# Gate pass of a hybrid decoder trunk: the skip's factor on GpSimd, and weight splits one half step later

## The chip, the cores and the metric

The kernel runs on one core of a Trainium2 chip. The metric is the device time of one execution in microseconds (us). A core has TensorE (PE, with its weight loads as PEld), VectorE (DVE), ScalarE (ACT), GpSimd (POOL) and SyncE (SP). Each runs its own list of instructions in a fixed order, and semaphores make one engine wait for another. In this kernel SP and ACT issue the DMAs.

## The reference

One layer on x of 4096 x 1024 float32. After an RMSNorm, one projection gives five streams; two head groups use them, and a second projection joins them.

```python
u = rmsnorm(x, norm_w)
pool_x, pool_z, m_x, m_z, m_o = split(u @ w_in)            # 1024 columns each
y_pool = pool_mixer(pool_x) * silu(pool_z)
xc = silu(causal_conv(m_x));  h = mlstm_chunkwise(...)     # 4 heads of 256
h  = sigmoid(m_o) * h
hn = (h - mean(h)) * rsqrt(var(h) + EPS) * mh_norm_w       # per head
y_mlstm = (hn + m_skip * xc) * silu(m_z)
out = rmsnorm(x + concat(y_pool, y_mlstm) @ w_out)
```

The edit touches `m_skip * xc` and the preparation of the weights of the large products.

## The kernel before

The kernel has three stages: the pooling group (to about 755 us), the mLSTM (to about 1727 us), and a function `drive` that runs four *block-product passes*. The passes are, in order, `p_out1` (the pooling half of the output projection, to 2062 us), `p_o` (the *gate pass*, m_o, to about 2464 us), `p_z` (m_z, to about 2768 us) and `p_out2` (the mLSTM half of the output projection). Each pass is a product by Strassen's scheme with NP = 7 block products. It goes over NR = 4 rows r of 1024 positions; in each r over the seven products i, and in each product over two *half steps* kh. One half step is 24 matmuls, three for each product of a float32 pair, because every operand is split into a rounded high part and the rest: `split` casts on ScalarE (L104) and subtracts on VectorE (L105). A pass has 56 half steps.

In a half step `drive` issues the load of a later left operand (sr, L212, on ACT's queue), splits the one loaded before (L104, L105), emits the 24 matmuls (L111 to L113), lets each item finish with the product's result, and runs what has been deferred. `defer(fn, n)` puts `fn` on a list, and `run_deferred` counts it down once in each half step and runs it when n reaches zero. `load` allocates a weight's slot, issues the DMA of its sums (L161; a raw block is loaded by L154 before) and defers its split by one half step. This happens for the weights missing in the first r of the first pass, and in the last r of each pass for the next pass's seven.

In the gate pass, Head items make h for 128 positions and 512 channels: the gate's Tanh on ACT (L1067), times h (L1069, DVE), statistics (L1076, L1077, DVE), then for two items together rs = var + 4 EPS (L1082, DVE), its power -1/2 (L1083, POOL), nb = -mean x rs (L1085, DVE), and the normalisation h x rs + nb in place (L1090, ACT, four per pair). When a quarter of r is done, `heads_ready` gives four pairs of functions, one for each block of 128 channels. `fetch` loads xc into a tile of the ring xu (L1107, SP) and defers its multiplication by the channel's skip (L1108); `finish`, later, transposes the normalised h on PE (L1115) and adds the two on DVE (L1117: transposed x mh_norm_w + skip part). The result is stored by L184. Besides, `right_sums` makes sums of the next pass's weights: four loads (L132, SP), four additions on POOL (L138, L140, L143, L145), in r = 0 to 2 of the gate pass.

The program's order on each engine is not written by hand: a scheduler places the instructions on each engine by its own estimate, so the order after an edit is read from the built program. Within an engine's list nothing overtakes.

Of the kernel before, what the change touches and what calls it, by code (L numbers as in the profile page):

```python
# [11 lines left out]
AF = mybir.ActivationFunctionType  # L12
ALU = mybir.AluOpType
# [41 lines left out]
def tile_hybrid(  # L55
# [16 lines left out]
    nc = tc.nc  # L72
# [17 lines left out]
    msk = col[:, 56:64]  # L90
# [12 lines left out]
    def split(raw, hi, lo, eng=None):  # L103
        nc.scalar.copy(out=hi, in_=raw)  # L104
        (eng or nc.vector).tensor_tensor(out=lo, in0=raw, in1=hi.bitcast(F32), op=ALU.subtract)  # L105

    def mm3(ps, pairs, start=True, stop=True, skip=False):

        n = len(pairs)
        for k, (a, b) in enumerate(pairs):  # L110
            nc.tensor.matmul(ps, lhsT=a[0], rhs=b[0], start=start and k == 0, stop=False, skip_group_check=skip)  # L111
            nc.tensor.matmul(ps, lhsT=a[0], rhs=b[1], start=False, stop=False, skip_group_check=skip)  # L112
            nc.tensor.matmul(ps, lhsT=a[1], rhs=b[0], start=False, stop=stop and k == n - 1, skip_group_check=skip)  # L113
# [56 lines left out]
    def defer(fn, n=1):  # L170
        deferred.append([n, fn])

    def run_deferred():
        due = []
        for d in deferred:
            d[0] -= 1
            if d[0] <= 0:
                due.append(d)
        for d in due:
            deferred.remove(d)  # L180
            d[1]()

    def store(dst, t):
        defer(lambda: nc.sync.dma_start(out=dst, in_=t))  # L184
# [15 lines left out]
    def drive(passes, ring, slot_pool, tile, psp, background, first):  # L200


        steps = [(n, r, i, kh) for n in range(len(passes)) for r in range(NR) for i in range(NP) for kh in range(2)]
        got = {}

        def issue(t):
            if t >= len(steps):
                return
            n, r, i, kh = steps[t]
            hi = ring.tile([P, 2, T], F32R, name="sr")  # L210
            lo = ring.tile([P, 2, T], F32R, name="sr")
            nc.scalar.dma_start(out=lo.bitcast(F32), in_=passes[n].left[r][i][:, 2 * kh:2 * kh + 2, :])  # L212
            got[t] = hi, lo

        def make(t):
            if len(first) <= t < len(steps):
                hi, lo = got[t]
                split(lo.bitcast(F32), hi, lo)

        def load(p, i):  # L220
            def splits(todo):
                for f in todo:
                    f()

            todo = p.load(i, *slot_pool(i))
            defer(lambda: splits(todo))


        later, fetched = [], []
        banks = {}  # L230

        def prefetch():
            while later and len(fetched) < 4:
                get, use = later.pop(0)
                get()
                fetched.append(use)

        for t, pairs in enumerate(first):
            got[t] = tuple([pair[v] for pair in pairs] for v in range(2))
        assert len(first) == AHEAD - 1  # L240
        for t, (n, r, i, kh) in enumerate(steps):
            p = passes[n]
            issue(t + AHEAD - 1)
            if n + r == 0:
                miss = [v for v in range(NP) if v not in p.slots]
                if miss:
                    p.fetch(miss[0], tile)
                    load(p, miss[0])
            make(t + AHEAD - 2)
            s = got.pop(t)  # L250
            w = p.slots[i]
            if kh == 0 and i in (0, 1, 4):
                for q in range(4):
                    banks["abc"[(0, 1, 4).index(i)], q] = psp.tile([P, T], F32, name="ps")
            chain = "abab" "cbc"[i]
            if t % 14 == 0:
                for it in p.items:
                    it.begin(r)
            for q in range(4):
                ps = banks[chain, q]  # L260
                pairs = []
                for k in range(2):
                    kk = 2 * kh + k
                    sk = tuple(z[k] if isinstance(z, list) else z[:, k] for z in s)
                    if p.by_row:
                        pairs.append((tuple(z[:, q * P:(q + 1) * P] for z in sk), tuple(z[:, kk, :] for z in w)))
                    else:
                        pairs.append((tuple(z[:, kk, q * P:(q + 1) * P] for z in w), sk))
                mm3(ps, pairs, start=kh == 0 and i in (0, 1, 4), stop=kh == 1, skip=True)
                if kh == 1:  # L270
                    p.items[q].after(r, i, ps)
            if kh == 1:
                later.extend(p.ready(r, i) or ())
            run_deferred()
            if r + 1 == NR and n + 1 < len(passes):
                if kh == 0 and i:
                    load(passes[n + 1], i - 1)
                if kh == 1 and i < NP - 1 or (kh, i) == (0, NP - 1):
                    passes[n + 1].fetch(i, tile)
                if kh == 1 and i == NP - 1:  # L280
                    load(passes[n + 1], i)
            m = t % 14
            if m in FREE_BANKS:
                for _ in range(FREE_BANKS[m]):
                    if fetched:
                        fetched.pop(0)()
            prefetch()
            background(n, r, m)
        while later or fetched:
            prefetch()  # L290
            run_deferred()
            fetched.pop(0)()
        while deferred:
            run_deferred()
# [85 lines left out]
    with tc.tile_pool(name="a_st", bufs=4) as stp, \  # L380
# [147 lines left out]
        for b in range(NB):  # L528
# [6 lines left out]
            for j in range(NJ):  # L535
# [22 lines left out]
                if b == 0:  # L558
# [4 lines left out]
                                               op0=ALU.mult, op1=ALU.subtract)  # L563
# [22 lines left out]
    with tc.tile_pool(name="b_mx", bufs=NJ) as mxp, \  # L586
# [7 lines left out]
        def x_tile(dt=F32):  # L594
            return xu.tile([P, T], dt, name="xu")
# [404 lines left out]
    with tc.tile_pool(name="c_ring", bufs=8) as ring, \  # L1000
# [8 lines left out]
        class Sum(Item):  # L1009
# [5 lines left out]
            def get(self, r, rh, ch):  # L1015
                t = self.tile()
                nc.sync.dma_start(out=t, in_=self.src[rows_of(r, rh, self.q), ch * T:(ch + 1) * T])
                return t
# [74 lines left out]
        def heads_ready(r, i):  # L1093

            if i not in (2, 4, 5, 6):
                return
            rh, ch = {2: (0, 0), 4: (1, 1), 5: (1, 0), 6: (0, 1)}[i]
            name = {2: "c11", 4: "u3", 5: "s1", 6: "u2"}[i]
            hn = [getattr(it, name) for it in p_o.items]

            def turned(jj):
                j = 4 * ch + jj
                got = []

                def fetch():
                    sk = x_tile()
                    nc.sync.dma_start(out=sk, in_=xc_d[2 * r + rh][j])  # L1107
                    defer(lambda: nc.scalar.activation(out=sk, in_=sk, func=AF.Copy, scale=msk[:, j:j + 1]))  # L1108
                    got.append(sk)

                def finish():
                    sk, = got
                    tp = psp.tile([P, T], F32, name="ps")
                    for q in range(NCH):
                        nc.tensor.transpose(out=tp[:, q * P:(q + 1) * P], in_=hn[q][:, jj * P:(jj + 1) * P],  # L1115
                                            identity=ident)
                    nc.vector.scalar_tensor_tensor(out=sk, in0=tp, scalar=mhw[:, j:j + 1], in1=sk,  # L1117
                                                   op0=ALU.mult, op1=ALU.add)
                    store(hs_d[2 * r + rh][j], sk)

                return fetch, finish

            return [turned(jj) for jj in range(4)]
# [79 lines left out]
        def slot_pool(i):  # L1203
            return (w1p, "w1") if i < 4 else (w2p, "w2")
# [34 lines left out]
        def background(n, r, m):  # L1239
            if (n, r) == (0, 1) and m in (1, 3, 5, 7, 9, 11) or (n, r) == (0, 2) and m in (1, 3):  # L1240
                next(more)
            if n < 3 and m in (((2, 5, 8, 11), (), (6, 9, 11, 13), ()) if n == 0 else
                               ((1, 4, 7, 10), (1, 4), (1, 4), ()))[r]:
                next(weights[n])
            if (n, r, m) == (3, 0, 2):
                for h in range(2):
                    fw.append(x_tile())
                    nc.sync.dma_start(out=fw[h], in_=final_w[:, h * T:(h + 1) * T].partition_broadcast(P))
# [57 lines left out]
```

## Time and profile before

| what | value |
|---|---|
| median of 3 runs | 3108.35 us (3103.76 to 3109.62) |
| the profiled execution | 3106.23 us |
| its span | 3104.5 us |
| granted TensorE clock, mean | 0.972 |
| busy: PE, DVE, ACT, POOL | 2903.6, 2116.8, 1352.9, 883.5 us |
| TensorE's busy time, 1727.7 to 2062 (`p_out1`) | 309.08 of 334.30 us |
| 2062 to 2446 (gate pass) | 349.93 of 384 us |
| 2446 to 2768 (`p_z` and the gate pass's end) | 313.17 of 322 us |
| 2768 to 3093 (`p_out2`) | 310.26 of 325 us |

A row of the timeline gives the start, the duration, the engine and line, output <- input, how many instructions are joined in it, and in brackets how long the engine was idle before and what released it. A row of the waits gives the engine and what it wanted, what it waited for, and the total, the number and the longest of the waits. The sum of the profiled execution's idle and busy time is its span; the remaining 1.7 us lie around it.

### The profile page before, as it was taken

The numbers are of one execution on the slowest core, as the hardware profiler recorded it, in microseconds if no ns is written. First come the engines' busy times: TensorE is split into PE (matmuls) and PEld (weight loads), VectorE is DVE, ScalarE is ACT, GpSimd is POOL, SyncE is SP. The second block draws the span as 40 slices with busy tenths as digits, with TensorE's granted clock in tenths as the row PEclk, the third lists the DMA queues.
The fourth block names the chain that finished last, engine by engine and source line by source line (L and its number), as shares of the span: only waits on it lengthen the run. The fifth ranks groups of instructions, "written<-read, shape, count | busy, mean of one in ns | idle before, by whom it ended". The sixth has DMA issues, their size and how long they took to land. (4 is left out here: it accounts for less than half of the span.)

```text
span 3104.5 us, 45002 instructions
## 1 busy us (share of the span) xinstructions
PE 2903.6 (94%) x15912; PEld 2520.3 (81%) x15912; DVE 2116.8 (68%) x4172; ACT 1352.9 (44%) x2658; POOL 883.5 (28%) x924
## 2 busy tenths in 40 slices
PE   7999999998899999999998898998999999989998
PEld 6888888887889989989997676886777778867887
DVE  6555555554688888888889644567667766676666
ACT  4222122221676676767767311245556633343332
POOL 1122333333244454444443231002011133220000
PEclk9999999998999999999999999999999999999999
DMA  6344455546221121111212788676677888886664
GB/s 214 113 158 157 160 186 187 186 149 199 82 67 50 49 69 49 61 57 48 66 59 92 250 281 288 218 256 218 228 238 247 268 270 279 277 285 207 202 210 169
DMA packets 258002, 531.59 MB, mean 171 GB/s; under 512 B 28528, under 2 KB 72048, under 8 KB 257776
## 3 DMA queue, kind: packets, MB, share of 16 engines
q1 hardware_dynamic: 225952, 412.84, 38.4%
q10 hardware_dynamic: 31824, 115.88, 12.2%
q8 instruction: 125, 2.05, 0.3%
q14 instruction: 101, 0.83, 0.1%
HBM read 331.49 MB, written 197.13 MB: 170 GB/s over the span
## 5 line engine op out<-in xcount | busy, mean ns | idle before, releaser
L111 PE MATMUL ps<-w,sr 128*128 128x512 f32 x1320 | 523.5, 397 | 27.0 <-ACT sr L104 18.5
L113 PE MATMUL ps<-w,sr 128*128 128x512 f32 x1320 | 520.4, 395 | 18.5 <-DVE sr L105 18.5
L112 PE MATMUL ps<-w,sr 128*128 128x512 f32 x1320 | 521.1, 395 | 0.0
L105 DVE TENSOR_TENSOR sr<-sr 128x1024 fp32r<-128x1024 f32 x221 | 284.9, 1292 | 302.2 <-ACT sr L104 301.5
L104 ACT CAST sr<-sr 128x1024 fp32r<-128x1024 f32 x221 | 231.2, 1047 | 535.0 <-PE ps L112 255.3
L111 PE MATMUL acc<-u,w 128*128 128x512 f32 x1024 | 399.3, 390 | 1.6 <-ACT u L104 1.6
L112 PE MATMUL acc<-u,w 128*128 128x512 f32 x1024 | 399.3, 390 | 0.0
L113 PE MATMUL acc<-u,w 128*128 128x512 f32 x1024 | 399.2, 390 | 0.0
L111 PEld LDWEIGHTS ps<-w,sr 128*128 128x128 f32 x1320 | 252.3, 191 | 82.2 <-ACT sr L104 22.3
L113 PEld LDWEIGHTS ps<-w,sr 128*128 128x128 f32 x1320 | 251.3, 190 | 74.5 <-DVE sr L105 22.2
L111 PE MATMUL acc<-xu,w 128*128 128x256 f32 x992 | 296.4, 299 | 0.0
L112 PEld LDWEIGHTS ps<-w,sr 128*128 128x128 f32 x1320 | 251.7, 191 | 52.4 <-issue 0.5
L113 PE MATMUL acc<-xu,w 128*128 128x256 f32 x992 | 283.3, 286 | 0.0
L112 PE MATMUL acc<-xu,w 128*128 128x256 f32 x992 | 283.3, 286 | 0.0
L666 POOL TENSOR_TENSOR cs<-c,cs 128x516 fp32r<-128x516 f32 x124 | 179.8, 1450 | 240.0 <-ACT cs L665 214.4
L678 DVE SCALAR_TENSOR_TENSOR xc<-mx,col,xc 128x256 f32<-128x256 f32 x384 | 226.2, 642 | 15.2 <-ACT xc L760 11.5
L111 PEld LDWEIGHTS acc<-u,w 128*128 128x128 f32 x1024 | 192.3, 188 | 42.3 <-ACT u L104 2.4
L113 PEld LDWEIGHTS acc<-u,w 128*128 128x128 f32 x1024 | 192.4, 188 | 40.1
L112 PEld LDWEIGHTS acc<-u,w 128*128 128x128 f32 x1024 | 192.4, 188 | 40.0
L111 PEld LDWEIGHTS acc<-xu,w 128*128 128x128 f32 x992 | 192.7, 194 | 1.2
L112 PEld LDWEIGHTS acc<-xu,w 128*128 128x128 f32 x992 | 192.8, 194 | 0.0
L113 PEld LDWEIGHTS acc<-xu,w 128*128 128x128 f32 x992 | 192.2, 194 | 0.1
(230 smaller groups left out, 5927.9 us busy)
## 6 DMA issues: line engine op xcount, KB each, us to landing
sr<-us_d ACTq DMA_DIRECT2D x112, 512.0 KB, 5.1
us_d<-st SPq DMA_DIRECT2D x64, 512.0 KB, 2.7
sr<-ym_d ACTq DMA_DIRECT2D x56, 512.0 KB, 4.3
sr<-yp_d ACTq DMA_DIRECT2D x53, 512.0 KB, 5.6
st<-in_x_t_dram SPq DMA_DIRECT2D x32, 512.0 KB, 6.0
yp_d<-sg SPq DMA_DIRECT2D x64, 256.0 KB, 2.9
st<-us_d SPq DMA_DIRECT2D x32, 512.0 KB, 5.9
xu<-us_d SPq DMA_DIRECT2D x64, 256.0 KB, 3.6
```

Source lines behind the costliest of these rows:

```text
L104: nc.scalar.copy(out=hi, in_=raw)
L105: (eng or nc.vector).tensor_tensor(out=lo, in0=raw, in1=hi.bitcast(F32), op=ALU.subtract)
L111: nc.tensor.matmul(ps, lhsT=a[0], rhs=b[0], start=start and k == 0, stop=False, skip_group_check=skip)
L112: nc.tensor.matmul(ps, lhsT=a[0], rhs=b[1], start=False, stop=False, skip_group_check=skip)
L113: nc.tensor.matmul(ps, lhsT=a[1], rhs=b[0], start=False, stop=stop and k == n - 1, skip_group_check=skip)
L666: nc.gpsimd.tensor_tensor(out=t[:, 1], in0=cst[h], in1=t[:, 0].bitcast(F32), op=ALU.subtract)
L678: nc.vector.scalar_tensor_tensor(out=a[:, t], in0=m[:, t, i:i + TB], scalar=conv_w[:, jj * 4 + i:jj * 4 + i + 1], in1=a[:, t], op0=ALU.mul ...
```

## The change

The skip's multiplication L1108 (64 instructions in the gate pass) goes from ScalarE to GpSimd, and the deferred split of a weight runs two half steps after its load is issued instead of one. Nothing else is edited. Lines after the skip's grow by one (L1117 is L1118 in the changed kernel).

```diff
             todo = p.load(i, *slot_pool(i))
-            defer(lambda: splits(todo))
+            defer(lambda: splits(todo), 2)
...
                     nc.sync.dma_start(out=sk, in_=xc_d[2 * r + rh][j])
-                    defer(lambda: nc.scalar.activation(out=sk, in_=sk, func=AF.Copy, scale=msk[:, j:j + 1]))
+                    defer(lambda: nc.gpsimd.tensor_scalar(out=sk, in0=sk, scalar1=msk[:, j:j + 1], scalar2=None,
+                                                          op0=ALU.mult))
                     got.append(sk)
```

On GpSimd, in r = 1 of the gate pass (xu is the tile of skip x xc, rs the variance whose power is taken; + stands in the changed kernel alone, the other rows in both):

```order
 L1083 TENSOR_TENSOR rs_22523<-rs_22523,nhalf_70 128x4
+L1108 TENSOR_SCALAR xu_22714<-xu_22714,col_68 128x512
+L1108 TENSOR_SCALAR xu_22716<-xu_22716,col_68 128x512
 L1083 TENSOR_TENSOR rs_22611<-rs_22611,nhalf_70 128x4
+L1108 TENSOR_SCALAR xu_22718<-xu_22718,col_68 128x512
+L1108 TENSOR_SCALAR xu_22720<-xu_22720,col_68 128x512
 L1083 TENSOR_TENSOR rs_22652<-rs_22652,nhalf_70 128x4
+L1108 TENSOR_SCALAR xu_22828<-xu_22828,col_68 128x512
+L1108 TENSOR_SCALAR xu_22830<-xu_22830,col_68 128x512
+L1108 TENSOR_SCALAR xu_22832<-xu_22832,col_68 128x512
+L1108 TENSOR_SCALAR xu_22879<-xu_22879,col_68 128x512
 L1083 TENSOR_TENSOR rs_22756<-rs_22756,nhalf_70 128x4
```

Between two powers there now stand two or four skip factors, and r = 0 and r = 2 have the same rows with other numbers.

On ScalarE at the same place, before:

```order
L1090 ACTIVATE ch_22038<-ch_22038,nb_22614,rs_22611 128x256 x2
L1090 ACTIVATE ch_22046<-ch_22046,nb_22614,rs_22611 128x256 x2
L1067 ACTIVATE ch_22062<-ch_22062 128x512
L104 CAST sr_22661<-sr_22662 128x1024
L1108 ACTIVATE xu_22714<-xu_22714,col_68 128x512
L1108 ACTIVATE xu_22716<-xu_22716,col_68 128x512
L1108 ACTIVATE xu_22718<-xu_22718,col_68 128x512
L212 DMA sr_22835<-us_d2_74 128x1024
L1108 ACTIVATE xu_22720<-xu_22720,col_68 128x512
L1067 ACTIVATE ch_22148<-ch_22148 128x512
L1090 ACTIVATE ch_22054<-ch_22054,nb_22655,rs_22652 128x256 x2
L1090 ACTIVATE ch_22062<-ch_22062,nb_22655,rs_22652 128x256 x2
```

and on ScalarE there after the change:

```order
L1067 ACTIVATE ch_22062<-ch_22062 128x512
L1090 ACTIVATE ch_22038<-ch_22038,nb_22614,rs_22611 128x256 x2
L1090 ACTIVATE ch_22046<-ch_22046,nb_22614,rs_22611 128x256 x2
L104 CAST sr_22661<-sr_22662 128x1024
L212 DMA sr_22835<-us_d2_74 128x1024
L1090 ACTIVATE ch_22054<-ch_22054,nb_22655,rs_22652 128x256 x2
L1090 ACTIVATE ch_22062<-ch_22062,nb_22655,rs_22652 128x256 x2
```

The four skip factors are gone from between the two normalisations, and a Tanh stands ahead of the first.

On VectorE between the two nb of this group, before (the L1117 are the sums behind earlier transposes, sr a left operand's split):

```order
L1085 SCALAR_TENSOR_TENSOR nb_22614<-mv_22590,rs_22611 128x4
L1076 BN_STATS stats_22631<-ch_22054 128x6
L1077 BN_AGGR mv_22590<-stats_22631 128x2
L105 TENSOR_TENSOR sr_22574<-sr_22574,sr_22573 128x1024
L1077 BN_AGGR mv_22590<-stats_22631 128x2
L1117 SCALAR_TENSOR_TENSOR xu_22532<-ps_22690,col_68,xu_22532 128x512
L1117 SCALAR_TENSOR_TENSOR xu_22534<-ps_22696,col_68,xu_22534 128x512
L1069 SCALAR_TENSOR_TENSOR ch_22062<-ch_22062,xu_22513 128x512
```

and on VectorE after:

```order
L1085 SCALAR_TENSOR_TENSOR nb_22614<-mv_22590,rs_22611 128x4
L1077 BN_AGGR mv_22590<-stats_22631 128x2 x2
L105 TENSOR_TENSOR sr_22574<-sr_22574,sr_22573 128x1024
L1069 SCALAR_TENSOR_TENSOR ch_22062<-ch_22062,xu_22513 128x512
L1118 SCALAR_TENSOR_TENSOR xu_22532<-ps_22690,col_68,xu_22532 128x512
```

L1069 now stands ahead of both sums; nb stays ahead of the subtraction of sr and of L1069. Further down, the subtraction of the next sr (sr_22662) went from ahead of the second power's L1082 to behind the second nb.

On VectorE at the start of the first pass (w_ is a weight, L1026 adds a product to rows of x):

```order
+L105 TENSOR_TENSOR sr<-sr 128x1024
+L1026 TENSOR_TENSOR ch<-ps,ch 128x512 x12
 L105 TENSOR_TENSOR w_18892<-w_18892,w_18891 128x1024 x2
 L105 TENSOR_TENSOR sr<-sr 128x1024
-L1026 TENSOR_TENSOR ch<-ps,ch 128x512 x12
-L105 TENSOR_TENSOR w_18955<-w_18955,w_18954 128x1024
-L105 TENSOR_TENSOR sr<-sr 128x1024
-L105 TENSOR_TENSOR w_18955<-w_18955,w_18954 128x1024
-L105 TENSOR_TENSOR sr<-sr 128x1024
```

The twelve L1026 now come ahead of the two halves of a weight, where before the next weight's halves stood behind them with a left operand's split between.

## The prediction

> **What bounds the kernel now.** I read the page's head first, then the stretches of the block-product passes, then the waits of the gate pass and the timeline where TensorE stops in it.
>
> ```profile
> PE 2903.6 (94%) x15912; PEld 2520.3 (81%) x15912; DVE 2116.8 (68%) x4172; ACT 1352.9 (44%) x2658; POOL 883.5 (28%) x924
> ```
>
> TensorE is busy 94% of the span, so no edit here can win more than TensorE's idle time, and none can cost more than it makes TensorE wait. The gate pass runs from about 2062 to 2464 us; the windows below are two stretches of it, each about as long as one r (us, PE busy, PEld, DVE, ACT, POOL, granted clock, DMA share, GB/s).
>
> ```profile
> 2160.00:2255.00 95.00, 86.77 (x400) 71.98 (x399) 64.09 (x138) 49.70 (x81) 14.43 (x12) 0.96 0.69 227
> 2255.00:2352.00 97.00, 86.57 (x397) 71.70 (x396) 64.93 (x148) 51.58 (x83) 14.07 (x12) 0.95 0.71 232
> ```
>
> 8 to 10 us of each are TensorE's idle time; ScalarE is half idle, GpSimd nearly empty. No engine's load sets the time here; the order of dependent steps does. The waits between 2062 and 2446 us (total, times, longest) and the skip factor's own groups say which:
>
> ```profile
> POOL rs L1083 <- DVE rs L1082: 165.2, 16, 32.8
> ACT ch L1090 <- DVE nb L1085: 57.6, 23, 7.2
> DVE nb L1085 <- POOL rs L1083: 35.4, 30, 6.1
> PE ps L1115 <- ACT ch L1090: 27.1, 14, 5.6
> L1108 ACT ACTIVATE xu<-xu,col x64: 706/718/741, 2035.4 to 2465.3; 128x512 f32<-128x512 f32 x64
>   DMA xu<-xc_d: 40.2, 15
> DMA to landing us min/median/max: 2.6/4.8/7.7
> ```
>
> TensorE's stops are nearly all transposes (L1115) waiting for the normalisation (L1090): 27.1 us. That hangs on nb (L1085), which hangs on the power on GpSimd (L1083). The last three lines are the skip factor: 64 x 0.718 = 46 us of ScalarE, and 40.2 us in which ScalarE stood before it because its input, loaded by L1107, takes 4.8 us to land.
>
> **Moving the skip factor.** ScalarE loses 46 us of work and 40.2 us of waiting. GpSimd gets both, and GpSimd is where the power stands. So the order on GpSimd decides, not its load. It has two skip factors ahead of rs_22611 and two ahead of rs_22652, where before the powers followed each other directly. The r = 1 group before, ScalarE, then GpSimd, SyncE, VectorE and TensorE:
>
> ```profile
> 2244.66 1.95 ACT L1108 ACTIVATE xu<-xu,col 128x512 f32<-128x512 f32 x3
> 2249.86 0.72 ACT L1108 ACTIVATE xu<-xu,col 128x512 f32<-128x512 f32 x1 [3.25 <-DMA xu<-xc_d]
> 2251.00 2.06 ACT L1090 ACTIVATE ch<-ch,nb,rs 128x256 f32<-128x256 f32 x4
> ...
> 2239.98 1.01 POOL L1083 TENSOR_TENSOR rs<-rs,nhalf 128x4 f32<-128x4 f32 x1 [7.35 <-DVE rs L1082]
> 2248.18 1.01 POOL L1083 TENSOR_TENSOR rs<-rs,nhalf 128x4 f32<-128x4 f32 x1 [7.19 <-DVE rs L1082]
> 2266.07 1.26 POOL L145 TENSOR_TENSOR xu<-xu 128x512 f32<-128x512 f32 x1
> ...
> 2236.39 3.03 SPq L1107 DMA_DIRECT2D xu<-xc_d  x3
> 2244.72 0.32 SPq L1107 DMA_DIRECT2D xu<-xc_d  x1
> ...
> 2241.02 0.16 DVE L1085 SCALAR_TENSOR_TENSOR nb<-mv,rs 128x4 f32<-128x4 f32 x1 [0.88 <-POOL rs L1083]
> 2242.72 1.38 DVE L1117 SCALAR_TENSOR_TENSOR xu<-ps,col,xu 128x512 f32<-128x512 f32 x2
> 2244.01 0.68 DVE L1069 SCALAR_TENSOR_TENSOR ch<-ch,xu 128x512 f32<-128x512 f32 x1
> 2246.74 1.20 DVE L105 TENSOR_TENSOR sr<-sr 128x1024 fp32r<-128x1024 f32 x1
> ...
> 2251.64 0.55 PE L1115 MATMUL ps<-ident,ch 128*128 128x128 f32 x3 [3.28 <-ACT ch L1090]
> ```
>
> *Price of one skip factor on GpSimd.* No such instruction stands in the trace. The ends are ScalarE's 0.72 us and GpSimd's addition of two tiles of the same 128x512 at 1.26 us (L145); I take 1.26, the row of the same engine, and keep 0.72 for the range. The Trainium skill ("GPSIMD Engine Reference", section 4.1) calls one-input operations on GpSimd roughly line rate; by its 1.03 cycles an element (section 3.1) an estimate is 0.44 us, and the sum below would be +8 instead of +13. No run so far shows which.
>
> *First power.* Of the three loads issued from 2236.39 on within 3.03 us, the second goes out near 2237.9 and lands 4.8 us later, at 2242.7. Then the skip factor (1.26) and the power (1.01): 2245.0, where the power before ended at 2240.99. So nb comes 4.0 us late, and VectorE stands behind it, since nb keeps its place in VectorE's order. From nb to the end of L1069 (ch_22062) VectorE took 2241.02 to 2244.69 = 3.67 us, and the two L1117 there (1.38) now come after it: 2.3. L1069 ends at about 2247.3, 2.6 us late.
>
> *The load behind it.* The fourth L1107 (xu_22720) takes the buffer that this L1069 reads last; before it went out at 2244.72, right behind it. Now it goes at 2247.4 and, with the same 5.1 us to ScalarE's release at 2249.86, lands at 2252.5.
>
> *Second power.* rs_22652 could run at 2248.18 before; now it stands behind the skip factor of xu_22720: 2252.5 + 1.26 + 1.01 = 2254.8, nb 0.16, L1090 at 2255.0 against 2251.00. TensorE's stop of 3.28 us becomes about 7.3: +4.0. With 0.72 us a skip factor it is about +2.7, and where the landing is a little later, +5. The subtraction of sr (1.20) that now stands behind nb ends near 2256.2; TensorE needs it some 1 us after its first transpose at 2255.6, so it adds nothing to 0.5.
>
> The same order stands in r = 0 and r = 2, and the trace has the same stop there:
>
> ```profile
> 2153.14 0.72 ACT L1108 ACTIVATE xu<-xu,col 128x512 f32<-128x512 f32 x1 [3.68 <-DMA xu<-xc_d]
> 2154.93 0.90 PE L1115 MATMUL ps<-ident,ch 128*128 128x128 f32 x3 [5.59 <-ACT ch L1090]
> 2346.67 0.72 ACT L1108 ACTIVATE xu<-xu,col 128x512 f32<-128x512 f32 x1 [3.73 <-DMA xu<-xc_d]
> 2348.46 0.55 PE L1115 MATMUL ps<-ident,ch 128*128 128x128 f32 x3 [3.75 <-ACT ch L1090]
> ```
>
> In each, ScalarE's skip factor waits for the same late load, so the load's lateness (2.6) and the longer tail behind its landing (1.4) carry over: 3 x 4.0 = +12.0.
>
> *The second stop of r = 0 and r = 1.* There the last power stands behind the four right-sum additions on GpSimd:
>
> ```profile
> 2261.55 1.88 POOL L138 TENSOR_TENSOR xu<-xu 128x512 f32<-128x512 f32 x1 [3.43 <-DMA xu<-in_w_in_dram]
> 2269.18 0.47 PE L1115 MATMUL ps<-ident,ch 128*128 128x128 f32 x1 [4.88 <-ACT ch L1090]
> ```
>
> The loads of these additions follow the next L1107s on SyncE's queue, and those wait for buffers that VectorE frees after nb. All of it moves with the 4.0; what comes on top is between nothing and the 1.20 us of the subtraction that is now behind nb. I take 0.8: +1.6 for both.
>
> *r = 3.* Two powers follow each other without a skip factor between in most groups, which is better than r = 0 to 2; but the last two have five and three ahead:
>
> ```profile
> 2452.43 1.34 ACT L1108 ACTIVATE xu<-xu,col 128x512 f32<-128x512 f32 x2 [0.85 <-DMA xu<-xc_d]
> 2452.54 1.01 POOL L1083 TENSOR_TENSOR rs<-rs,nhalf 128x4 f32<-128x4 f32 x1 [9.28 <-DVE rs L1082]
> ```
>
> The power ready at 2452.54 waits for the landings to about 2453 and two skip factors: about 3 us late. Against that stand the stops that ScalarE's skip factors lengthen there. I put it at 0, between -4 and +5.
>
> **The weights' splits.** They are the same instructions, one half step (24 matmuls) later. A weight is used several half steps behind its load, so the later finish is hidden; its cover is gone only if the load lands as late as its use. What moves is the order at the start of the first pass:
>
> ```profile
> 1750.11 0.69 DVE L1026 TENSOR_TENSOR ch<-ps,ch 128x512 f32<-128x512 f32 x1 [0.79 <-DMA ch<-in_x_dram]
> 1752.47 1.22 DVE L105 TENSOR_TENSOR w<-w,w 128x1024 fp32r<-128x1024 f32 x1 [1.67 <-ACT w L104]
> 1753.62 1.22 DVE L105 TENSOR_TENSOR sr<-sr 128x1024 fp32r<-128x1024 f32 x1
> 1754.89 0.50 PE L113 MATMUL ps<-w,sr 128*128 128x512 f32 x1 [4.73 <-DVE sr L105]
> ```
>
> Now two weight subtractions whose data is long there stand between L1026 and that sr: 1750.8 + 2 x 1.15 = 1753.1 instead of 1753.62. That is -0.5, between 0 and -1.5; at the other three pass borders I count nothing, between -2 and +2.
>
> **Sum.** 12.0 + 1.6 + 0 - 0.5 = +13, on the profiled execution's 3106.23 us: 3119.3. The median of the runs shown is 2.1 us above that execution; I say 3120.
>
> **Rivals.** *Faster.* If the loads are there when GpSimd reaches them, the powers aren't held and ScalarE's part of the stops goes: L1090 stood until 2251.00 behind ScalarE's skip factor though the power was done at 2249.19, 1.8 us, and as much in r = 0 and r = 2 by the same pattern, 5.4; with r = 3 at -4 and the splits at -0.5 that is -10: about 3096. For it speaks that ScalarE's waits are real (40.2 us); against it that the load of xu_22720 can't start before a buffer is freed, and lands 4.8 us later. It decides where the load lands before about 2246.9, so that the power still starts at 2248.18.
>
> *No change.* The stops keep their lengths, because ScalarE's gain of about 2 us in each offsets a power held only about 2 us longer: 3104 to 3111. It needs the first power's delay not to reach L1107, that is, VectorE to have other work ready ahead of nb.
>
> *Slower still, by VectorE.* A VectorE operation on two tiles takes much longer beside one on GpSimd:
>
> ```profile
> 2764.92 0.68 DVE L1149 TENSOR_TENSOR ch<-ch,xu 128x512 f32<-128x512 f32 x1
> 2774.33 1.75 DVE L1149 TENSOR_TENSOR ch<-ch,xu 128x512 f32<-128x512 f32 x1
> 2773.77 1.77 POOL L1167 TENSOR_TENSOR xu<-xu,ch 128x512 f32<-128x512 f32 x1
> ```
>
> The pass has many such operations:
>
> ```profile
> L105 DVE TENSOR_TENSOR sr<-sr 128x1024 fp32r<-128x1024 f32 x57 | 70.5, 1236 | 56.6 <-ACT sr L104 56.2
> L1069 DVE SCALAR_TENSOR_TENSOR ch<-ch,xu 128x512 f32<-128x512 f32 x60 | 39.9, 677 | 9.6 <-ACT ch L1067 6.9 <-ACT ch L1061 2.6
> ```
>
> GpSimd's 64 x 1.26 = 81 us of new work lie over about a fifth of the pass; of these 117 about 23 would meet one and lose up to 1.07 us each: 25 us of VectorE, perhaps a quarter of it on the chain, +6: 3126. The Trainium skill ("SBUF — State Buffer", section "Who interferes with whom") says that a VectorE instruction with two SBUF inputs and a GpSimd one that reads SBUF share a port and lock each other out for a whole instruction; these rows agree.
>
> **Numbers.** Forecast 0.50 (3113 to 3125), slower by VectorE too 0.12 (to 3132), no change 0.17, faster 0.21. A measurement of this kernel tells about 0.2%, 6.2 us, from nothing. Faster by more 0.21, within 0.17, slower 0.62. The range 3098 to 3130 leaves out the better half of the faster case and the far end of the slowest.
>
> **What would show it.** L1083's waits turn from VectorE to GpSimd's own skip factors and their loads; the sum of L1115's waits for L1090 rises from 27.1 to about 40; the stops at 2154.93, 2251.64 and 2348.46 grow by about 4 us each; ScalarE waits longer for nb. If those stops shrink instead, the step that fails is the power standing behind a load that hasn't landed; if they grow but the end doesn't move, it is r = 3 and the later passes. A w subtraction that TensorE waits for would prove the splits wrong.

## The result, and the profile after

The changed kernel takes 3143.19 us (median of 4 runs, 3139.57 to 3146.44) against 3108.98 us for the kernel before on the same chip: ratio 1.0109, 95% interval 1.0096 to 1.0122. It is 34 us slower. Slower was forecast, but by 13 us, and 3143 lies outside the range of 3098 to 3130.

The page of the kernel after, its span and its first section:

```profile
span 3142.7 us, 45010 instructions
PE 2914.4 (93%) x15912; PEld 2526.3 (80%) x15912; DVE 2125.3 (68%) x4172; ACT 1315.4 (42%) x2594; POOL 997.3 (32%) x988
```

ScalarE lost 37.5 us of work, GpSimd gained 114 us. The span is 38.2 us longer, TensorE's busy time only 11, for the same 15912 instructions at a mean granted clock of 0.967 instead of 0.972. Where the 38 us arise is read by matching the same matmul in both traces; the difference of its two start times is called the lag. Here is the first matmul after a stop in the first pass, then the first of r = 1, 2 and 3 of the gate pass, then the first of the pass behind it, in the kernel before:

```profile
1893.96 0.80 PE L111 MATMUL ps<-w,sr 128*128 128x512 f32 x1 [13.67 <-ACT sr L104]
...
2155.48 0.78 PE L111 MATMUL ps<-w,sr 128*128 128x512 f32 x1
...
2251.95 0.48 PE L111 MATMUL ps<-w,sr 128*128 128x512 f32 x1
...
2348.76 0.48 PE L111 MATMUL ps<-w,sr 128*128 128x512 f32 x1
...
2444.84 0.80 PE L111 MATMUL ps<-sr,w 128*128 128x512 f32 x1
```

and in the kernel after, with the two long stops that follow the last of them:

```profile
1900.23 0.80 PE L111 MATMUL ps<-w,sr 128*128 128x512 f32 x1 [14.93 <-ACT sr L104]
...
2169.16 0.77 PE L111 MATMUL ps<-w,sr 128*128 128x512 f32 x1
...
2274.00 0.78 PE L111 MATMUL ps<-w,sr 128*128 128x512 f32 x1
...
2376.86 0.78 PE L111 MATMUL ps<-w,sr 128*128 128x512 f32 x1
...
2478.61 0.61 PE L111 MATMUL ps<-sr,w 128*128 128x512 f32 x1
...
2500.11 1.95 PE L1116 MATMUL ps<-ident,ch 128*128 128x128 f32 x7 [4.14 <-ACT ch L1090]
...
2509.19 0.79 PE L111 MATMUL ps<-sr,w 128*128 128x512 f32 x1 [3.97 <-DVE xu L1118]
```

The lag is 6.3 us in the first pass, then 13.7, 22.1, 28.1 and 33.8, and about 42 after the last two stops; some 4 come back later. So r = 0, 1 and 2 cost 7.4, 8.4 and 6.0 us, and r = 3 with the border behind it 14. The 6.3 of the first pass can't be put down to the change: the run with the splits alone has about the same lag there (5.7), but its median is no longer, and runs whose splits are those of before lie between 0.8 us ahead and 7.4 us behind at this matmul.

For r = 1, from the first matmul shown for it to the one shown for r = 2, the busy times before and after (us, PE busy, PEld, DVE, ACT, POOL, granted clock, DMA share, GB/s):

```profile
2155.48:2251.95 96.47, 88.24 (x403) 72.93 (x401) 65.56 (x147) 51.17 (x82) 14.44 (x12) 0.95 0.68 226
2169.16:2274.00 104.84, 89.99 (x403) 74.17 (x401) 67.29 (x147) 41.61 (x67) 44.08 (x29) 0.91 0.64 211
```

Of the 8.4 us, 6.6 are idle time of TensorE, and 1.8 are the same 403 instructions at a lower clock.

The waits of the gate pass after (2062 to 2490 us; total, times, longest), and the skip factor's own groups:

```profile
POOL xu L1108 <- DMA xu<-xc_d: 147.9, 17, 23.6
DVE nb L1085 <- POOL rs L1083: 62.5, 30, 7.2
PE ps L1116 <- ACT ch L1090: 36.2, 19, 6.3
PE ps L1116 <- DVE xu L1118: 10.9, 3, 4.4
...
L1108 POOL TENSOR_SCALAR xu<-xu,col 128x512 f32<-128x512 f32 x64 | 113.8, 1790 | 174.6 <-DMA xu<-xc_d 160.7 <-DVE sr L105 12.5 <-DVE rs L1082 1.5
L1108 POOL TENSOR_SCALAR xu<-xu,col x64: 1559/1576/2599, 2041.7 to 2495.7; 128x512 f32<-128x512 f32 x64
```

The transposes' waits for the normalisation rose from 27.1 to 36.2 (27.3 where the window before also runs to 2490), and a wait for VectorE's sums (L1118) of 10.9 came. VectorE now stands 62.5 us at nb for the power, 35.4 before. A skip factor takes 1.576 us on GpSimd: longer than GpSimd's addition of two tiles (1.26), more than twice ScalarE's 0.718.

The rows of the group of r = 1 whose order stands above, for GpSimd, SyncE, VectorE, ScalarE and TensorE:

```profile
2257.21 3.12 POOL L1108 TENSOR_SCALAR xu<-xu,col 128x512 f32<-128x512 f32 x2 [10.13 <-DMA xu<-xc_d]
2260.29 1.04 POOL L1083 TENSOR_TENSOR rs<-rs,nhalf 128x4 f32<-128x4 f32 x1
2261.32 1.57 POOL L1108 TENSOR_SCALAR xu<-xu,col 128x512 f32<-128x512 f32 x1
2267.72 1.57 POOL L1108 TENSOR_SCALAR xu<-xu,col 128x512 f32<-128x512 f32 x1 [4.83 <-DMA xu<-xc_d]
2269.25 1.04 POOL L1083 TENSOR_TENSOR rs<-rs,nhalf 128x4 f32<-128x4 f32 x1
...
2250.84 13.20 SPq L1107 DMA_DIRECT2D xu<-xc_d  x4
...
2254.10 0.16 DVE L1082 TENSOR_SCALAR rs<-mv 128x4 f32<-128x4 f32 x1
2261.37 0.16 DVE L1085 SCALAR_TENSOR_TENSOR nb<-mv,rs 128x4 f32<-128x4 f32 x1 [6.46 <-POOL rs L1083]
2263.01 0.68 DVE L1069 SCALAR_TENSOR_TENSOR ch<-ch,xu 128x512 f32<-128x512 f32 x1
...
2270.53 2.08 ACT L1090 ACTIVATE ch<-ch,nb,rs 128x256 f32<-128x256 f32 x4 [5.95 <-DVE nb L1085]
...
2264.50 0.66 PE L1116 MATMUL ps<-ident,ch 128*128 128x128 f32 x2 [3.52 <-DVE xu L1118]
2271.18 0.48 PE L1116 MATMUL ps<-ident,ch 128*128 128x128 f32 x1 [6.02 <-ACT ch L1090]
2274.57 0.63 PE L112 MATMUL ps<-w,sr 128*128 128x512 f32 x1
2275.00 0.63 PE L113 MATMUL ps<-w,sr 128*128 128x512 f32 x1
```

The first power's input was there at 2254.3 (L1082); the power ran at 2260.29, behind two factors that waited for a load until 2257.2. VectorE stood for it until 2261.37. Only then came L1069, which frees the buffer of the fourth load, so that the four loads take SyncE 13.2 us. That load let its factor start at 2267.72, and the second power ran at 2269.25. TensorE stops twice, 3.52 and 6.02 us, where it stopped once for 3.28.

### The profile page after: what moved, and what is told of

It is laid out like the page before. It is cut to its first block, busy times and chain, and to the rows that moved or that the text cites. A ratio compares the mean times of both kernels' runs of the same rounds, so it can differ in the third digit from the quotient of the medians.

```text
span 3142.7 us, 45010 instructions
## 1 busy us (share of the span) xinstructions
PE 2914.4 (93%) x15912; PEld 2526.3 (80%) x15912; DVE 2125.3 (68%) x4172; ACT 1315.4 (42%) x2594; POOL 997.3 (32%) x988
## 5 line engine op out<-in xcount | busy, mean ns | idle before, releaser
L105 DVE TENSOR_TENSOR sr<-sr 128x1024 fp32r<-128x1024 f32 x221 | 287.5, 1303 | 301.6 <-ACT sr L104 301.1
L104 ACT CAST sr<-sr 128x1024 fp32r<-128x1024 f32 x221 | 231.4, 1048 | 577.7 <-PE ps L112 297.9
```

## The experiments

Theory A says that the loss comes because the power stands on GpSimd's list behind factors that wait for loads. Its rivals are GpSimd's work and its slowing of VectorE, and the splits. Ratios are to the kernel before on the same chip.

**The two parts apart.** The splits alone keep L1108 on ScalarE; the skip factor alone keeps `defer(lambda: splits(todo))`.

> Only the split of a weight two half steps behind its load; the skip factor stays on ScalarE. Theory A (the loss is GpSimd's order): the gate pass is as before, the first pass costs the 5 us by which the changed kernel fell behind in it (its lag on the kernel before goes from 0.75 us at the pass's start to 6.27 at its fifth product of r = 1), so 3111 to 3115 us, ratio 1.001 to 1.002. Theory B (the splits carry much of the loss, since they reorder the loads at every pass border): 3120 or more. Theory C (the lag in the first pass is chance of the loads' landings): 3109, ratio within 0.001 of 1.

Measured: 3108.86 us, ratio 1.0003 (0.9991 to 1.0016).

> Only the skip factor on GpSimd; the splits one half step behind their load as before. Theory A: nearly the whole loss, 3134 to 3141 us, with stops of about 6 us at the transposes of r = 0, 1 and 2 (3.3 to 5.6 before). Theory B: under 3125. If the two parts add up, this run and the one with the splits alone together lose the 34 us of the change; if not, they act on each other at the gate pass's end, where the order of the last r differs.

Measured: 3142.25 us, ratio 1.0107 (1.0089 to 1.0125). The skip factor alone loses as much as the whole change, a little more than the 3134 to 3141 us expected. In its profiled execution the same matmuls give 6.5, 7.1 and 6.6 us for r = 0, 1 and 2 and 13 for r = 3 with the border. The splits show no effect, which is theory C of the first expectation; their interval, some -3 to +5 us, can't tell the prediction's -0.5 us from nothing.

**The factor's length.** The edit on top of the skip factor alone:

```diff
-nc.gpsimd.tensor_scalar(out=sk, in0=sk, ...)
+nc.gpsimd.tensor_scalar(out=sk[:, 0:4], in0=sk[:, 0:4], ...)
```

> The skip factor on GpSimd over 4 of its 512 columns (the other 508 keep xc unscaled), in the same order on GpSimd as in the changed kernel, splits as before. It waits for the same loads but works less. Theory A1 (the power is held by the wait for the load): each of r = 0 to 2 still loses about 4 to 5 us, 3120 to 3128 us in all. Theory A2 (the power is held by GpSimd's work, 1.576 us a factor): the loss is gone, 3100 to 3111 us, the stops at the transposes at or under those of before.

Measured: 3121.33 us, ratio 1.0046 (1.0030 to 1.0062). The factor on GpSimd then takes

```profile
L1108 POOL TENSOR_SCALAR xu<-xu,col x64: 288/296/1332, 2042.9 to 2481.5; 128x4 f32<-128x4 f32 x64
```

The order on GpSimd is that of the run with the skip factor alone. So 14 of its 33 us are there with a factor of almost no work (A1), and 19 come with its length (A2): 1.28 us less a factor saves 19 us, an estimate of 15 us for each microsecond. The time lies in A1's range, but neither theory is right alone.

**Later, full width:** `defer(..., 3)` in place of one half step.

> The skip factor on GpSimd, full width, but deferred three half steps behind its load instead of one; splits as before. GpSimd's list then has the two first powers of a quarter ahead of its skip factors. Theory A1 (a power stands behind a factor whose load hasn't landed): the stops of 6 us in r = 0 to 2 go back to those of before or less, since ScalarE is also free of its waits: 3098 to 3111 us. Theory A2 (GpSimd's work of 64 x 1.576 us, and VectorE slowed beside it): the work is the same, so most of the loss stays, above 3122 us.

Measured: 3136.78 us, ratio 1.0098 (1.0082 to 1.0114). It doesn't tell the theories apart: up to eight factors in a row still stand ahead of a power, and with three half steps part of the factors comes only after L1118 and then multiplies the sum, so it waits for sums and stores and holds the tile longer. In its waits the factor stands for them:

```profile
POOL xu L1108 <- DMA hs_d<-xu: 44.3, 6, 9.7
POOL xu L1108 <- DVE xu L1118: 27.5, 6, 7.1
```

**No power on GpSimd.** `nc.vector.reciprocal(out=rs, in_=rs)` takes the power's place and leaves the square root out, with the factor on GpSimd and, as a control, on ScalarE.

> Skip factor on GpSimd in its full width, splits as before, and the power replaced by a reciprocal on VectorE (the square root is left out), so that no power stands on GpSimd. The factors wait for the same loads and take the same 1.57 us. Theory A (a power behind factors): the loss goes, 3095 to 3110 us, and L1085 no longer waits for GpSimd. Theory B (GpSimd's work delays the factors' own use, L1118, or slows VectorE): a good part stays, 3118 or more.

> The control for the run without the power: reciprocal on VectorE in place of the power, skip factor on ScalarE as in the kernel before. Both theories: faster than before by the power's 1 us and its two hand-overs at the 5 to 6 stops that hang on it, 3097 to 3105 us. Theory A: within 6 us of the run with the factor on GpSimd; theory B: 10 us or more under it.

Measured: 3077.93 us with the factor on GpSimd, ratio 0.9897 (0.9884 to 0.9910), and 3078.88 us with it on ScalarE, 0.9900 (0.9885 to 0.9915). Moving the factor costs nothing when no power is on GpSimd, though the factors wait for their loads as before (181.9 us, against 147.9 in the changed kernel). The waits of the two from 2062 to 2490 us, the factor on GpSimd first:

```profile
POOL xu L1108 <- DMA xu<-xc_d: 181.9, 12, 30.8
PE ps L1116 <- ACT ch L1090: 6.0, 8, 2.1
```

```profile
PE ps L1115 <- ACT ch L1090: 8.6, 9, 2.1
```

This speaks for theory A, and against GpSimd's work as such, which is the same here. It also shows what the prediction hadn't asked and what neither expectation had (3095 us at the least): the kernel before gains some 31 us where a reciprocal on VectorE takes the place of the power on GpSimd. The reciprocal also shortens the chain, which the runs with the power on VectorE below do not.

**The factor on VectorE** (`nc.vector.tensor_scalar`).

> The skip factor on VectorE instead of ScalarE or GpSimd, splits as before, power on GpSimd. VectorE's list has the factors behind nb in the tight groups (xu_22714 to 22720 behind nb_22759), so no power and no nb is held by a load there. Theory A: no loss like the change's, 3100 to 3115 us: ScalarE is free, but the factors stand ahead of other work of VectorE and delay the sums. Theory B (freeing ScalarE is what hurts, since its casts then run early and the loads crowd): 3125 or more.

Measured: 3111.68 us, ratio 1.0012 (1.0000 to 1.0023). The factor takes 0.481 us there and waits 37.6 us for the same loads, but stands behind the nb of the tight groups, and there is no loss like the change's. Freeing ScalarE is not what hurts.

**No factor at all.**

> The skip factor left out (xc goes in unscaled), splits as before: what freeing ScalarE is worth at most, with nothing put on GpSimd. Theory A: the stops before the transposes lose ScalarE's part, about 2 us in each of r = 0 to 2 and up to 4 in r = 3: 3097 to 3103 us. If ScalarE's waits were hidden: 3106 to 3110.

Measured: 3104.94 us, ratio 0.9982 (0.9970 to 0.9993), 5.6 us by the ratio; the time lies between the two expectations. This is all that ScalarE's freedom was worth; the faster rival had 10.

**nb on GpSimd**, so that VectorE doesn't stand for the power, with the factor on ScalarE, on GpSimd, and on VectorE:

```diff
-nc.vector.scalar_tensor_tensor(out=nb, in0=mv[:, two, :, 0], scalar=-1.0, in1=rs, op0=ALU.mult, op1=ALU.mult)
+nc.gpsimd.tensor_tensor(out=nb, in0=mv[:, two, :, 0], in1=rs, op=ALU.mult)
+nc.gpsimd.tensor_scalar(out=nb, in0=nb, scalar1=-1.0, scalar2=None, op0=ALU.mult)
```

> nb moved from VectorE to GpSimd, right behind the power (a product and a multiplication by -1, 128x4 each), skip factor on ScalarE and splits as before. VectorE then no longer stands at nb for the power. Theory A (a queue's head that waits holds what is behind it): VectorE's 36.8 us of waits at nb go, the sums, subtractions and L1069 behind it come earlier, the stops shrink: 3085 to 3104 us. Theory B (only the length of the chain from the statistics to the normalisation counts): the chain gets two GpSimd steps of about 0.3 to 0.6 us and loses one hand-over, so 3105 to 3115.

> As the run with nb on GpSimd, and the skip factor on GpSimd too, splits as before. The power is still behind factors that wait, but VectorE isn't. If the change's loss comes through VectorE's blocked list (the fourth load waits for L1069, which waits for nb): 3100 to 3118. If it comes by the power's lateness alone, through ScalarE's normalisation to the transposes: 3122 or more.

> nb on GpSimd, skip factor on VectorE, splits as before: nothing that waits for a load stands ahead of a power, and ScalarE is free. Theory A: the fastest of the correct ones, 3085 to 3103 us. Theory B: as the kernel before or slower, 3106 to 3120.

Measured: 3117.08 us, ratio 1.0030 (1.0016 to 1.0045), with the factor on ScalarE; 3127.19 us, 1.0056 (1.0038 to 1.0074), on GpSimd; 3116.66 us, 1.0018 (1.0006 to 1.0030), on VectorE. The first lies above both expectations: VectorE's waits at nb go, but the two operations (0.39 us each in the mean, 0.20 and 0.23 in the median) lengthen the chain. ScalarE's normalisation waits 74.7 us for nb instead of 57.6, the transposes 34.5 us for the normalisation instead of 27.3. The third is no faster than the first, as its theory B had it.

The second lies in the range set for the power's lateness alone (3122 or more). But that range was set from the kernel before, and nb on GpSimd is at 3117 without the factor's move. Against that run the move costs 0.26%, 8 us (10 by the medians), instead of 33. This points to VectorE standing at nb for much of the loss; how much is not shown, because the scheduler also put one factor instead of two ahead of the first power here.

**The power on VectorE,** by a start value from an integer shift and two or three Newton steps, so that GpSimd's list drops out of the chain without the chain getting shorter:

```diff
-nc.gpsimd.tensor_tensor(out=rs, in0=rs, in1=nhalf..., op=ALU.pow)
+nc.vector.tensor_single_scalar(out=ry.bitcast(I32), in_=rs.bitcast(I32), scalar=1, op=ALU.arith_shift_right)
+nc.vector.tensor_scalar(out=ry.bitcast(I32), in0=ry.bitcast(I32), scalar1=-1.0, scalar2=float(0x5f3759df), op0=ALU.mult, op1=ALU.add)
+for it in range(2):
+    nc.vector.tensor_tensor(out=ra, in0=ry, in1=ry, op=ALU.mult)
+    nc.vector.scalar_tensor_tensor(out=ra, in0=ra, scalar=-0.5, in1=rs, op0=ALU.mult, op1=ALU.mult)
+    nc.vector.scalar_tensor_tensor(out=ry, in0=ra, scalar=1.5, in1=ry, op0=ALU.add, op1=ALU.mult)
```

> The power computed on VectorE instead of GpSimd: a start value by an integer shift and two Newton steps (8 small operations of 128x4, about 0.08 to 0.16 us each), skip factor on ScalarE and splits as before. Theory A (the cost of the power is GpSimd's queue and the hand-overs): most of the 30 us that the reciprocal gained stays, 3080 to 3095 us. Theory B (the cost is the length of the chain, which this doesn't shorten much: 0.7 to 1.3 us against 1.0 and two hand-overs): 3098 to 3112.

> As before it with three Newton steps (11 small operations). Each step adds some 0.25 to 0.5 us to the 32 chains: 3 to 10 us more than with two steps by both theories.

> The power by two Newton steps on VectorE and the skip factor on GpSimd, splits as before: the change's own part with nothing behind it on GpSimd that the chain needs. Theory A (the power behind the factors is the whole loss): within 6 us of the run with the factor on ScalarE. Theory B (the factor's own lateness and GpSimd's 1.57 us count too): 10 us or more above it.

Measured: two steps 3096.59 us, ratio 0.9959 (0.9947 to 0.9972); three steps 3100.83 us, 0.9978 (0.9966 to 0.9991); two steps and the factor on GpSimd 3097.79 us, 0.9966 (0.9954 to 0.9979). The third step costs 0.19%, 6 us, as expected. With the power off GpSimd the factor's move costs 0.07%, 2 us, within both intervals. With the runs of the reciprocal this is the main proof of theory A: the factors stand on GpSimd and wait for their loads as before, and without a power behind them the loss is gone. By the ratio the version with two steps is about 13 us faster than the kernel before, and by the medians 47 us faster than the changed one. So of the 31 us that the reciprocal gained, about 13 remain, between theory A's 3080 to 3095 and theory B's 3098 to 3112. Where the other 18 went stays open. VectorE has the steps' work on top, and its list puts other work between them: from the end of L1082 to the start of nb it takes 5.5 us in the median, where it was 1.21 before and 0.71 with the reciprocal.

## Why the prediction was right or wrong

The direction and the mechanism were right: the power standing behind factors that wait for loads, nb late with it, L1069 and the fourth load behind nb. The size was wrong: r = 0 to 2 cost 21.8 us for a forecast of 13.6, and r = 3, put at 0, cost 14 with the border, of which some 4 came back. The terms follow.

*Price of a factor.* Taken 1.26 us with 1.26 as the upper end, measured 1.576. GpSimd's nearest row was not an upper bound. By the 15 us for each microsecond of the short-factor run, 0.31 us is about 5 of the missing 21. The Trainium skill ("GPSIMD Engine Reference", section 4.1) has one-input operations at roughly line rate; by the 1.03 cycles an element of its section 3.1 my estimate was 0.44 us. The measurement, 1.576 us for 512 elements in float32 with a scalar from a column, decides against it here.

*First power.* Forecast 4.0 us late, measured 6.0 (2254.3 to 2260.29). I counted one factor behind the second load's landing. But the first two loads land 0.5 us apart, and both factors, 3.12 us, lie behind the landings. These also came later than I took them: 6.2 and 6.1 us after their issue at 2250.84 and 2251.44, not 4.8. (Before, the second load went out at 2236.99 and took 6.0 us; my 2237.9 and 4.8 gave nearly the right landing by luck.)

*Second power.* The delay reaches the fourth load as forecast, 2.6 us then and about 5.3 now, and the normalisation comes at 2270.53, where the kernel before had it at 2251.00: 19.5, less the 13.7 of lag at the start of this r, is 5.8 us late, not 4.0. The sums behind nb also come late, which made a stop that the prediction didn't have (3.52 us at 2264.50). The same pair of stops stands in each r: together 10.6, 9.5 and 9.3 us for r = 0, 1 and 2, where there was one of 5.59, 3.28 and 3.75. The second stops of r = 0 and r = 1, forecast 0.8 us longer each, became shorter: 2.81 us for 3.15 and 2.19 for 4.88.

*The clock.* The prediction had no term for it. The granted clock is 0.50 from 2263.75 to 2277.41 us, around the two stops, and the matmuls from 2274.57 to 2277.13 come every 0.43 us, not 0.23, some 1.4 us in all. The Trainium skill ("TensorE: Matmul & The Clock Gate", Part 1) says that the clock halves after about 3.4 us of idle time and returns after about as much work; the halving agrees with these rows, while the return came here some 5 us after the transposes went on at 2272.16. From r = 0 to the border TensorE is busy 7.5 us longer for the same work (438.8 us from 2062 to 2540 before, 446.3 from 2068.47 to 2581 after), a part of the lag that isn't idle time.

*r = 3.* Taken 0, between -4 and +5, measured 14 with the border. This is the step that failed most. The rows of the last two powers after:

```profile
2481.23 8.84 POOL L1108 TENSOR_SCALAR xu<-xu,col 128x512 f32<-128x512 f32 x5 [4.25 <-DMA xu<-xc_d]
2490.04 1.03 POOL L1083 TENSOR_TENSOR rs<-rs,nhalf 128x4 f32<-128x4 f32 x1
2491.07 3.12 POOL L1108 TENSOR_SCALAR xu<-xu,col 128x512 f32<-128x512 f32 x2
2495.68 2.55 POOL L1108 TENSOR_SCALAR xu<-xu,col 128x512 f32<-128x512 f32 x1 [1.48 <-DVE rs L1082]
2498.19 1.03 POOL L1083 TENSOR_TENSOR rs<-rs,nhalf 128x4 f32<-128x4 f32 x1
...
2484.67 0.15 DVE L1082 TENSOR_SCALAR rs<-mv 128x4 f32<-128x4 f32 x1
2491.10 0.66 DVE L1085 SCALAR_TENSOR_TENSOR nb<-mv,rs 128x4 f32<-128x4 f32 x1 [5.95 <-POOL rs L1083]
```

The five factors were in my own reading of the order, but I counted two of them, and set a gain of ScalarE's against them. They take 8.84 us in a row; the power ready at 2484.8 runs 5.2 us late. The next one, ready at 2495.7, runs 2.5 us late behind three more, and the stop of 4.14 us at 2500.11 hangs on it. The run without factors shows that ScalarE's whole gain over all four rs is 5.6 us.

These two powers don't explain the whole 14. The first 5.7 us of it arise earlier in r = 3, where the powers run as soon as their input is there (2426.73 and 2430.85). There ScalarE stood 13.1 us until 2417.14 at a weight's cast (L104) for its load, ahead of the cast of TensorE's next left operand; why these loads land later stays open.

*The splits.* Forecast -0.5, measured nothing (1.0003, 0.9991 to 1.0016). The term is too small for these runs to tell.

*Rivals.* Faster: the real part is 5.6 us, and needs the powers unheld. No change: out. Slower still by VectorE: its operations hardly changed, as its groups in the gate pass after show:

```profile
L105 DVE TENSOR_TENSOR sr<-sr 128x1024 fp32r<-128x1024 f32 x59 | 73.2, 1240 | 48.0 <-ACT sr L104 47.8
L1069 DVE SCALAR_TENSOR_TENSOR ch<-ch,xu 128x512 f32<-128x512 f32 x63 | 44.4, 717 | 3.9 <-ACT ch L1061 2.5 <-ACT ch L1067 1.3
```

1240 against 1236 ns and 717 against 677: 64 times 0.04 is under 3 us, not 25. The time went past that rival's 3126, but by another way. GpSimd's factors were lengthened instead: the mean one takes 1.79 us, the shortest 1.559. All 18 factors of 2.0 us or more overlap an L105 or an L1069 on VectorE by 0.65 us or more; of the 46 shorter ones seven do.

## What to carry to other kernels

An engine that is nearly idle can still be the wrong place for work: ask what short operation on its list others wait for, and put nothing that waits for a load ahead of it. When such a row of instructions stands ahead, count every one of them behind the landings, and look at each place of the order, the last row too. When TensorE's stops grow, count the time at the lower clock behind them as well. And when a small step sits on a slow hand-over in a tight chain, try moving that step, not the work around it: here the power's move gained about 13 us where the factor's lost 34.

## What the runs showed of the hardware

GpSimd took 1.576 us in the median for a one-tile product of 128x512 with a column scalar, more than for an addition of two tiles (1.26 us), 0.296 us for one of 128x4, and 1.01 us for a power of 128x4. VectorE did the 128x512 product in 0.481 us, and its operations of 128x4 in 0.15 to 0.17 us in the median. The granted clock stood at 0.50 for 13.7 us around two TensorE stops of 3.52 and 6.02 us.
